# Hybrid attention layer on one core: in the first chunk, maxima and copies taken crosswise, one more upper part on ScalarE, one small transpose a unit later

## The chip, the cores and the metric

The kernel runs on one core of one Trainium2 chip. Its engines are TensorE (PE, matrix products, with PEld for its weight loads), VectorE (DVE), ScalarE (ACT), GpSimd (POOL) and SyncE (SP, which here only issues transfers). The metric is device time in microseconds of one execution, lower is better. Before the change the median of 3 runs is 1146.15 us (1145.9 to 1146.28).

## The reference, cut to what matters

One decoder layer over 2048 positions of width 1024. An adaLN vector (shift, scale, gate) comes from the condition `c`; the normalised input is scaled and shifted by it, projected once, and split over two attention branches.

```python
mod = jax.nn.silu(c) @ w_ada[l] + b_ada[l]
shift, scale, gate = jnp.split(mod, 3, axis=-1)
h = rms_norm(x, g_pre[l]) * (1.0 + scale[:, None, :]) + shift[:, None, :]
proj = h @ w_in[l]
qa, ka, va, fa, za, qb, kb, vb, zb = jnp.split(proj, split_points, axis=-1)
oa = forgetting_attention(qa, ka, va, fa + b_fgate[l]) * jax.nn.silu(za)
ob = sliding_window_sink_attention(rope(qb), rope(kb), vb, sinks[l]) * jax.nn.silu(zb)
y = jnp.concatenate([oa, ob], axis=-1) @ w_out[l]
x = x + gate[:, None, :] * rms_norm(y, g_post[l])
```

The change touches how `shift` becomes a column layout, how the first 512 rows of `h` are split into halves of lower precision, and when a maximum over the `zb` weights is gathered. What is computed stays the same.

## The kernel before, in words

Products keep nearly float32 precision with float16 operands: each operand is an upper part (`hi`, float16) and a rest (`lo`), and each product is three matmuls, hi by hi, hi by lo, lo by hi. The input is cut into four chunks of 512 rows (`ci` 0 to 3). For each chunk `turn(ci, k)` does one of eight column blocks: PE transposes four 128x128 tiles of the normalised rows into a PSUM bank `px`; ACT writes the scaled and shifted block as float32 (`hf`), and, where `high` is set, once more as float16 (the upper part, `hi`); else DVE makes the upper part by a cast (line 436). DVE then subtracts to get the rest (line 437). There are five `px` banks and three `hf` buffers. Both parts land in `hT[ci]`, which the projections read.

Ahead of it the start section runs in one fixed order per engine. `ada_two` multiplies the condition by `w_ada` into two PSUM banks, one for each half of 512 columns of the shift row (`pm[0][0]` is bank 1, `pm[0][1]` is bank 2). Line 628 takes the largest magnitude of each half on DVE, `ada_row` (line 512) copies each half out on ACT, `ada_turn` (line 516) transposes each half back **into the same bank** on PE, and `ada_col` (line 520) reads the transposed columns on DVE. The two maxima are joined (line 631), summed over quadrants by a matmul with `sel` (line 636), and give a bound `bm` (line 641), a power of two `pH`, and from it the scale `Gp` and shift `Shp` that every `turn` of chunk 0 needs.

Beside the turns DVE finds the maxima of the weights `zb0` and `zb1` (lines 659, 660). `z_row` and `z_all` gather them over the partitions with a transpose (line 997), a reduction (998), a scaling (999), a matmul (1002) and a copy to `mxs` (1003), all through bank 2. They hang on a list of units: unit n is the n-th group of projection matmuls. Units 0 to 7 are the `kb` projection of chunk 0 (line 335), 8 to 15 its `vb` projection (line 776, two 128-row blocks in bank 1, then two in bank 2), then come `zb0` and `zb1`. `at_slice(n, f)` issues `f` just ahead of unit n.

While that runs, ACT takes the sums of squares of chunk 1 (`squares(1)`, line 406), DVE makes its reciprocal root (`root(1)`, lines 92 to 106, at unit 9), and the rotary part of `kb` starts with a copy `qf` on ACT (line 723) and a product with the cosine on DVE (line 742). Each engine works off its instructions in order; two engines never read or write the same PSUM bank without a semaphore between them, reads included.

Of the kernel before, what the change touches and what calls it, by code (L numbers as in the profile page):

```python
# [15 lines left out]
ALU = mybir.AluOpType  # L16
AX = mybir.AxisListType
# [23 lines left out]
def hybrid_layer(  # L41
# [17 lines left out]
    V, A, G, PE, SP = nc.vector, nc.scalar, nc.gpsimd, nc.tensor, nc.sync  # L59
# [360 lines left out]
    def turn(ci, k):  # L420

        px = ps_x.tile([P, CH], F32, tag="x", name="px")
        for u in range(4):
            PE.transpose(px[:, u * P:(u + 1) * P], xt[ci * 4 + u][:, k * P:(k + 1) * P], ident[:])
        hf = hst.tile([P, CH], F32, tag="hf", name="hf")
        hi, lo = hT[ci][:, 0, k, :], hT[ci][:, 1, k, :]

        high = k % 2 == 0 if ci else k in (0, 4)

        def scaled():  # L430
            for dst in ([hi] if high else []) + [hf[:]]:
                A.activation(dst, px[:], AF.Identity, scale=Gp[:, k:k + 1], bias=Shp[:, k:k + 1])

        def split():
            if not high:
                V.tensor_copy(hi, hf[:])
            V.tensor_tensor(lo, hf[:], hi, op=ALU.subtract)

        return scaled, split

    def turn_x(ci, k):
        scaled, split = turn(ci, k)
        after(1, scaled)
        after(2, split)
# [12 lines left out]
    with tc.manual_schedule():  # L457
# [43 lines left out]
        pm = {1: [ps_x.tile([P, CH], F32, tag="x", name="pm") for _ in range(2)], 0: [bk[1], bk[2]]}  # L501
# [9 lines left out]
        def ada_row(half, n):  # L511
            A.activation(arow[half][:, n * CH:(n + 1) * CH], pm[half][n][:], AF.Copy)
# [112 lines left out]
            ada_two(0, k)  # L625
        rm = st.tile([P, 2], F32, name="rm")
        for n in range(2):
            V.tensor_reduce(rm[:, n:n + 1], pm[0][n][:], axis=AX.X, op=ALU.max, apply_absolute_value=True)
            ada_row(0, n)
        rmx = st.tile([P, 1], F32, name="rmx")  # L630
        V.tensor_reduce(rmx[:], rm[:], axis=AX.X, op=ALU.max)
        shf = col8("shf")
        turned = [turn(0, 0)]
        ada_turn(0, 0)
        turned.append(turn(0, 1))
        PE.matmul(bk[0][:, P:P + 1], sel[:], rmx[:], start=True, stop=True)
        ada_turn(0, 1)
# [352 lines left out]
    def at_slice(n, f):  # L990
        events.setdefault(n, []).append(f)
# [12 lines left out]
        for n in range(2):  # L1004
            wq[f"zb{n}"].append(mxs[:, 2 + n:3 + n])

    at_slice(8, z_row)
    at_slice(11, z_all)
    at_slice(9, lambda: root(1))
    for u in range(4):  # L1010
# [775 lines left out]
```

## Time and profile before

| what | value |
|---|---|
| median of 3 runs | 1146.15 us |
| the profiled execution's own time | 1144.82 us |
| its span | 1143.0 us |
| mean granted TensorE clock | 0.992 |
| DVE busy | 938.0 us (82%) |
| ACT busy | 692.2 us (61%) |
| POOL busy | 252.2 us (22%) |

The span is what the trace covers; 1.82 us of the execution's own time lie around it. Rows of the timeline give start and duration in us, engine, line, operation, tiles, a count, and in brackets how long the engine stood idle before and what released it. Starts are exact; the ends of matmuls are modelled, and two instructions of one engine can overlap a little where neither waits for the other.

### The profile page before, as it was taken

What the parts mean: (1) busy time and instruction counts of PE and PEld (TensorE: products, weight loads), DVE (VectorE), ACT (ScalarE), POOL (GpSimd) and SP (SyncE); (2) the same over time, 40 slices, a digit from 0 to 9 for tenths busy, and PEclk for the clock granted to TensorE, in tenths of its full rate; (3) what the DMA queues carried; (4) which work ended last, traced back from release to release, by engine and by line L of the source; (5) the groups of instructions that cost most, each with busy time, mean ns of one, the idle gap of its engine ahead of it and who ended that gap; (6) DMA issues with size and microseconds to landing.
All of it is one profiled execution on the core that took longest, in us unless ns stands there. A gap on an engine that the chain in (4) does not pass through costs nothing.

```text
span 1143.0 us, 26952 instructions
## 1 busy us (share of the span) xinstructions
PE 1102.7 (96%) x10386; PEld 638.2 (56%) x10386; DVE 938.0 (82%) x2331; ACT 692.2 (61%) x1177; POOL 252.2 (22%) x391
## 2 busy tenths in 40 slices
PE   5899999999999999999999999999999999999997
PEld 1466657654579855555555555555555554544443
DVE  6775668879899658789988889979888888988885
ACT  4666446656666534767767667777777677433331
POOL 2011122434443301122221221202111036100000
PEclk9999999999999999999999999999999998999999
DMA  9646426676787532343332332223212168478753
GB/s 332 224 139 171 106 71 135 117 159 126 153 164 141 108 66 71 71 100 81 75 78 70 98 85 64 62 54 87 52 40 61 29 167 216 131 186 215 192 163 111
DMA packets 210324, 136.35 MB, mean 119 GB/s; under 512 B 145276, under 2 KB 189348, under 8 KB 210196
## 3 DMA queue, kind: packets, MB, share of 16 engines
q1 hardware_dynamic: 198100, 98.53, 36.9%
q0 software_dynamic: 11616, 35.58, 11.1%
q8 instruction: 81, 1.33, 0.5%
q10 hardware_dynamic: 480, 0.53, 0.2%
q14 instruction: 47, 0.39, 0.1%
HBM read 62.58 MB, written 25.18 MB: 77 GB/s over the span
## 4 chain that ended last, share of the span: by engine, by line
PE 74%; DVE 11%; ACT 5%; DMA 5%; issue 4%; SPq 1%; POOL 0%; DVEq 0%; ACTq 0%; POOLq 0%
PE bk L335 28%; PE bk L1540 13%; PE bk L353 6%; PE sta L1345 5%; PE bk L1296 4%; PE sta L1346 4%; PE poa L1373 2%; PE poa L1374 2%; PE poa L1371 2%; DMA wa<-in_w_ada_dram 2%; PE bk L776 1%; DVE pha L1361 1%; PE pss L870 1%; PE pob L933 1%; DVE a_m L1299 1%
## 5 line engine op out<-in xcount | busy, mean ns | idle before, releaser
L1350 ACT ACTIVATE p<-sta,lift,scl_qk 128x1024 f32<-128x1024 f32 (+2 forms) x160 | 171.8, 1073 | 85.2 <-PE sta L1346 80.6
L335 PE MATMUL bk<-hT,wh_qk 128*128 128x512 f16 x768 | 198.0, 379 | 0.0
L1361 DVE TENSOR_TENSOR pha<-p,pha 128x1024 f16<-128x1024 f32 (+2 forms) x160 | 172.3, 1077 | 0.0
L1540 PE MATMUL bk<-wohl,oz 128*128 128x512 f16 (+2 forms) x792 | 170.2, 373 | 1.9 <-DVE wohl L1469 1.4
L1358 ACT ACTIVATE pha<-p 128x1024 f16<-128x1024 f32 (+2 forms) x160 | 148.2, 926 | 31.2 <-POOL p L1354 27.0
L1299 DVE TENSOR_REDUCE a_m<-bk 128x1 f32<-128x512 f32 x192 | 129.4, 683 | 36.7 <-PE bk L1296 36.2
L1540 PEld LDWEIGHTS <-oz 128*128 128x128 f16 x792 | 76.1, 99 | 87.3 <-issue 2.0
L1371 PE MATMUL poa<-vt,pha 128*128 128x65 f16 x1088 | 117.2, 193 | 2.1 <-DVE ona L1380 2.1
L1374 PE MATMUL poa<-vt,pha 128*128 128x65 f16 x1088 | 116.6, 193 | 0.8 <-DVE pha L1361 0.8
L1373 PE MATMUL poa<-vt,pha 128*128 128x64 f16 x1088 | 117.0, 195 | 0.0
L1345 PE MATMUL sta<-T 128*128 128x512 f16 (+1 forms) x320 | 109.9, 348 | 5.2 <-ACT p L1350 5.0
L1296 PE MATMUL bk<-T 66*128 66x512 f16 (+2 forms) x320 | 110.6, 349 | 0.9 <-DVE a_m L1301 0.5
L1371 PEld LDWEIGHTS <-pha 128*128 128x128 f16 x1088 | 101.9, 97 | 16.5 <-DVE ona L1380 2.9
L1373 PEld LDWEIGHTS <-pha 128*128 128x128 f16 x1088 | 101.4, 97 | 13.6
L335 PEld LDWEIGHTS <-wh_qk 128*128 128x128 f16 x768 | 70.1, 97 | 69.4 <-issue 0.6
L1346 PE MATMUL sta<-T 69*128 69x512 f16 (+1 forms) x320 | 108.3, 349 | 0.0
L1374 PEld LDWEIGHTS <-pha 128*128 128x128 f16 x1088 | 101.2, 99 | 1.2 <-DVE pha L1361 1.2
L335 PE MATMUL bk<-hT,wh_za 128*128 128x512 f16 x384 | 101.5, 382 | 0.0
L353 PE MATMUL bk<-wh_va,hT 128*128 128x128 f16 x1536 | 92.6, 219 | 0.0
L335 PE MATMUL bk<-hT,wh_zb 128*128 128x512 f16 x384 | 90.8, 379 | 0.0
L353 PEld LDWEIGHTS <-hT 128*128 128x128 f16 x1536 | 87.5, 98 | 4.9 <-issue 2.5
L1354 POOL TENSOR_SCALAR_AFFINE_SELECT p<-p 128x256 f32<-128x256 f32 x64 | 32.1, 502 | 258.1 <-ACT p L1350 247.4
(504 smaller groups left out, 1955.6 us busy)
## 6 DMA issues: line engine op xcount, KB each, us to landing
hT<-in_x_dram SPq DMA_DIRECT2D x20, 512.0 KB
wa<-in_w_ada_dram SPq DMA_DIRECT2D x16, 512.0 KB
T<-stq SPq DMA_DIRECT2D x128, 64.0 KB
T<-z_d SPq DMA_DIRECT2D x16, 512.0 KB
z_d<-tz POOLq DMA_DIRECT2D x30, 256.0 KB, 3.0
out_dram<-hT POOLq DMA_DIRECT2D x15, 512.0 KB, 5.7
xt<-in_x_dram SPq DMA_DIRECT2D x12, 512.0 KB
qs<-qf SPq DMA_DIRECT2D x80, 64.0 KB
```

Of the source, the lines that this page charges most:

```text
L335: PE.matmul(ps, whl[:, a, k, :], hT[ci][:, b, k, :], start=(k == 0 and n == 0), stop=(k == KT - 1 and n == 2))
L353: PE.matmul(ps[:, u * P:(u + 1) * P], hT[ci][:, a, k, u * P:(u + 1) * P], whl[:, b, k, :], start=(k == 0 and n == 0), stop=(k == KT - 1 an ...
L1296: PE.matmul(mx[:, :w], T[0:XM, 0, i * P:(i + 1) * P], T[0:XM, 2, pc * CH:pc * CH + w], start=True, stop=True)
L1345: PE.matmul(self.st[:, o:o + w], T[:, 3, kb_], T[:, 1, qc], start=True, stop=False)
L1346: PE.matmul(self.st[:, o:o + w], T[0:XR, 2, kb_], T[0:XR, 0, qc], start=False, stop=True)
L1350: A.activation(self.p32[:, :self.w], self.st[:, :self.w], AF.Exp, scale=scl[f"qk{self.hd}"][:], bias=lift[:])
L1358: A.activation(self.ph[:, 0, :self.w], self.p32[:, :self.w], AF.Copy)
L1361: V.tensor_tensor(self.ph[:, 1, :self.w], self.p32[:, :self.w], self.ph[:, 0, :self.w], op=ALU.subtract)
L1371: PE.matmul(po[:, u, :], ph[:, 0, pq], vt[:, b, hd, 0:65], start=(self.first and n == 0 and u == 0), stop=False)
L1373: PE.matmul(po[:, u, 0:64], ph[:, 0, pq], vt[:, b, hd, 65:VW], start=False, stop=False)
L1374: PE.matmul(po[:, u, :], ph[:, 1, pq], vt[:, b, hd, 0:65], start=False, stop=(self.last and n == len(self.blocks) - 1))
L1540: PE.matmul(py, self.hl[:, i, k, :], w_slot(8 * j + k)[:, cc], start=(k == 0 and m_ == 0), stop=(k == KT - 1 and m_ == 2))
```

## The change

Three edits. In `turn`, chunk 0 makes the upper parts of blocks 0, 3 and 6 on ACT, before of blocks 0 and 4. The maxima of the shift row are taken second half first, while the copies stay first half first. `z_row` hangs on unit 9, before on unit 8.

```diff
-        high = k % 2 == 0 if ci else k in (0, 4)
+        high = k % 2 == 0 if ci else k in (0, 3, 6)
...
         for n in range(2):
-            V.tensor_reduce(rm[:, n:n + 1], pm[0][n][:], axis=AX.X, op=ALU.max, apply_absolute_value=True)
+            V.tensor_reduce(rm[:, 1 - n:2 - n], pm[0][1 - n][:], axis=AX.X, op=ALU.max, apply_absolute_value=True)
             ada_row(0, n)
...
-    at_slice(8, z_row)
+    at_slice(9, z_row)
     at_slice(11, z_all)
     at_slice(9, lambda: root(1))
```

In the rows below `bk_139` is bank 1 and `bk_140` bank 2; the brackets name the engines whose semaphores an instruction waits for.

On PE, after the last products of `ada_two`, before the change: the last transpose of `turn(0, 0)`, the first half's `ada_turn`, the start of `turn(0, 1)`.

```order
L424 MATMUL px<-ident,xt_257 128x128 [waits Activation_49]
L516 MATMUL bk_139<-ident,arow_209 128x128 [waits Activation_49]
L516 MATMUL bk_139<-ident,arow_209 128x128 x3
L424 MATMUL px<-ident,xt_251 128x128
L424 MATMUL px<-ident,xt_253 128x128
```

The same place on PE after the change.

```order
L424 MATMUL px<-ident,xt_257 128x128 [waits Activation_49]
L516 MATMUL bk_139<-ident,arow_209 128x128 [waits DVE_49]
L516 MATMUL bk_139<-ident,arow_209 128x128 x3
L424 MATMUL px<-ident,xt_251 128x128
L424 MATMUL px<-ident,xt_253 128x128
```

The order is the same, but the first half's transposes wait for DVE, no longer for ACT. On DVE at that place, after the change:

```order
L628 TENSOR_REDUCE rm<-bk_140 128x1 [waits PE_49]
L628 TENSOR_REDUCE rm<-bk_139 128x1 [waits Activation_49]
L631 TENSOR_REDUCE rmx<-rm 128x1 [waits DVE_49]
L520 TENSOR_REDUCE shf<-bk_139 128x4 [waits PE_49]
L641 TENSOR_TENSOR bm<-bk_138,pre 128x1 [waits PE_49]
```

Bank 1 is read by ACT first and by DVE second, bank 2 the other way round; before, DVE read each bank first.

On ACT, the end of chunk 0's turns and what follows (`junk` is a square of chunk 1, `qf` the copy for the rotary part), with the change's rows marked:

```order
 L406 ACTIVATE junk_520,ss_516<-hT3_110 128x1024
 L406 ACTIVATE junk_522,ss_516<-hT3_110 128x1024
+L723 ACTIVATE qf_594<-bk0_138 128x512
 L406 ACTIVATE junk_524,ss_516<-hT3_110 128x1024
-L723 ACTIVATE qf_594<-bk0_138 128x512
 L416 ACTIVATE hT3_110<-hT3_110,rst_517 128x1024
```

`qf` has moved ahead of the last square of chunk 1. On PE, at the border between `kb` (line 335) and `vb` (line 776):

```order
 L335 LDWEIGHTS wh_kb_365
 L335 MATMUL bk0_138<-hT0_107,wh_kb_365 128x512
-L997 MATMUL bk2_140<-ident_120,mxs_130 2x128
 L776 LDWEIGHTS hT0_107
 L776 MATMUL bk1_139<-wh_vb_367,hT0_107 128x136
```

The transpose of the two weight maxima leaves this place and stands twelve `vb` matmuls later. SP and POOL keep their rows in the same order.

## The prediction

> **What bounds the kernel now.** I read the page's span and its chain of work first, then the waits and the timeline of the first 80 us, where all three edits lie.
>
> ```profile
> span 1143.0 us, 26952 instructions
> PE 74%; DVE 11%; ACT 5%; DMA 5%; issue 4%; SPq 1%; POOL 0%; DVEq 0%; ACTq 0%; POOLq 0%
> ```
>
> Three quarters of the chain that ended last are PE. From about 80 us on the chain hardly leaves PE, so what the first 80 us lose or gain moves the end by about as much. In there PE waits for others. The place of the second edit, engine by engine (DVE, ACT, PE):
>
> ```profile
> 36.83 0.69 DVE L628 TENSOR_REDUCE rm<-bk 128x1 f32<-128x512 f32 x1 [4.34 <-PE bk L508]
> 37.69 0.69 DVE L628 TENSOR_REDUCE rm<-bk 128x1 f32<-128x512 f32 x1 [0.17 <-PE bk L508]
> 38.41 0.15 DVE L631 TENSOR_REDUCE rmx<-rm 128x1 f32<-128x2 f32 x1
> 39.45 0.16 DVE L641 TENSOR_TENSOR bm<-bk,pre 128x1 f32<-128x1 f32 x1 [0.31 <-PE bk L636]
> 37.55 0.60 ACT L512 ACTIVATE arow<-bk 128x512 f32<-128x512 f32 x1 [3.23 <-DVE rm L628]
> 38.41 0.60 ACT L512 ACTIVATE arow<-bk 128x512 f32<-128x512 f32 x1 [0.26 <-DVE rm L628]
> 40.68 0.78 ACT L432 ACTIVATE hT<-px,Shp,Gp 128x512 f16<-128x512 f32 x1 [1.67 <-DVE shf L520]
> 37.58 0.66 PE L424 MATMUL px<-ident,xt 128*128 128x128 f32 x4
> 38.20 0.66 PE L516 MATMUL bk<-ident,arow 128*128 128x128 f32 x4
> 39.13 0.28 PE L636 MATMUL bk<-rmx,sel 128*128 128x1 f32 x2
> ```
>
> By what releases the two maxima, bank 1 is ready at 36.8 and bank 2 at 37.65. The chain runs: maximum of half 1, its copy (37.55), its transposes (38.20), the four of turn 1, the matmul with `sel`, `bm` at 39.45, first turned block at 40.68. Soon after it DVE becomes full. The first row is a stretch of 5 us (length, busy time and count of PE, PEld, DVE, ACT, POOL, granted clock, DMA share, GB/s), the others are DVE's timeline:
>
> ```profile
> 45.00:50.00 5.00, 3.33 (x14) 1.16 (x12) 4.90 (x10) 4.85 (x9) 0.00 (x0) 1.00 0.11 28
> 43.29 0.69 DVE L437 TENSOR_TENSOR hT<-hf,hT 128x512 f16<-128x512 f32 x1
> 43.90 0.42 DVE L436 CAST hT<-hf 128x512 f16<-128x512 f32 x1
> 44.35 0.69 DVE L437 TENSOR_TENSOR hT<-hf,hT 128x512 f16<-128x512 f32 x1
> 47.69 1.21 DVE L659 TENSOR_REDUCE mxs<-wr_zb 128x1 f32<-128x1024 f32 x1
> 48.82 0.42 DVE L436 CAST hT<-hf 128x512 f16<-128x512 f32 x1
> 50.33 0.69 DVE L437 TENSOR_TENSOR hT<-hf,hT 128x512 f16<-128x512 f32 x1
> 50.94 1.21 DVE L660 TENSOR_REDUCE mxs<-wr_zb 128x1 f32<-128x1024 f32 x1
> 52.97 0.15 DVE L92 TENSOR_SCALAR rs_v<-ss 128x4 f32<-128x4 f32 x1
> 56.71 0.15 DVE L1003 COPY mxs<-bk 128x2 f32<-128x2 f32 x1
> ```
>
> DVE is busy for 4.90 of 5 us. A cast costs it 0.45 us (43.90 to 44.35), a subtraction 0.61, a maximum of weights 1.13 (47.69 to 48.82). The root of chunk 1 starts at 52.97, `mxs` is copied at 56.71; on that hang the scale of the `zb0` weights, DVE's and ACT's work behind it, and so the turns of chunk 1. What closes the stretch:
>
> ```profile
> 78.94 0.38 PE L335 MATMUL bk<-hT,wh_kb 128*128 128x512 f16 x1 [0.39 <-DVE hT L436]
> 79.67 0.59 PE L335 MATMUL bk<-hT,wh_kb 128*128 128x512 f16 x2 [0.35 <-DVE hT L437]
> ```
>
> PE, on the last block of chunk 1's turns, waits 0.39 and 0.35 us for DVE. So the line over DVE and ACT sets the end of this stretch, and PE has about 0.7 us in hand against it.
>
> **The change part by part.** The sum is made against the profiled execution, 1144.82 us (span 1143.0 and 1.82 around it). It lies 1.33 under the median of 1146.15; I carry the difference over to the median.
>
> *Crosswise maxima.* ACT no longer waits for DVE: it copies half 1 from 36.83 on, 0.72 earlier, done at 37.43. DVE takes half 2 first, when bank 2 is ready, 37.69 as before. Then half 1: two reads in a row without a wait between them are 0.61 apart for this length (43.29 to 43.90), so from 38.30 to 38.99. Half 1's maximum is now the last reader of bank 1, and the order of the changed kernel shows the transposes into bank 1 waiting for DVE. They start at about 39.03 (0.04 for a hand-over, as from 38.15 to 38.20), not 38.20: **+0.83**. The joined maximum is ready at 39.02 + 0.15 = 39.17, before PE has come to the `sel` matmul, so it adds nothing. Behind the waiting transposes PE queues turn 1, `sel`, half 2's transposes and turns 2 to 4; `bm` waits for `sel`, and all turned blocks of chunk 0 wait for `bm`. From 38.20 to 40.68 nothing else in the chain changes, so the whole section moves by 0.83. If those transposes were not held, they could start once turn 0's four are through, no earlier than 38.0, and the `sel` matmul would still need the later maximum, 39.17 plus a hand-over of 0.04, which is 0.1 over its 39.13: the bounds are +0.1 and +0.9, and I take +0.83, since the wait stands in the order.
>
> [...]
>
> *Upper parts on ACT.* Blocks 3 and 6 lose their casts on DVE, block 4 gains one: of six, five are left. Counted from an unmoved start, up to the first weight maximum DVE has four casts before and after, so it starts at 47.69 as before. Block 6 then goes straight to its subtraction: from there DVE is 0.45 early, the last rest of chunk 0 starts at 49.88, the second weight maximum at 50.49. ACT makes eleven parts of chunk 0 (eight `hf`, three upper) where it made ten:
>
> ```profile
> 44.01 0.80 ACT L432 ACTIVATE hT<-px,Shp,Gp 128x512 f16<-128x512 f32 x1
> 44.67 0.80 ACT L432 ACTIVATE hf<-px,Shp,Gp 128x512 f32<-128x512 f32 x1
> 47.56 1.05 ACT L406 ACTIVATE junk<-hT 128x1024 bf16<-128x1024 f32 x1
> 51.10 1.06 ACT L406 ACTIVATE junk<-hT 128x1024 bf16<-128x1024 f32 x1
> 52.06 0.19 ACT L406 ACTIVATION_READ_ACCUMULATOR junk<-hT 128x1 f32 x1
> 52.16 0.58 ACT L723 ACTIVATE qf<-bk 128x512 f32<-128x512 f32 x1
> ```
>
> One part takes 0.66 (44.01 to 44.67). Ten from 40.68 would be through at 47.28, but the squares start at 47.56, so 0.28 are waits for DVE to free an `hf` buffer; with DVE's casts further apart these go. Eleven end at 47.94, and the squares start 0.4 later. In the changed order `qf` stands ahead of the fourth square: it starts 1.06 after the third one, as before after the fourth, and takes 0.48 (0.58 less the 0.1 by which rows overlap on ACT), where two squares are 1.18 apart: 1.54 - 1.18 = 0.36 more. The sum, ready before at 52.06 + 0.19 = 52.25, is ready at 53.01, and the root cannot start before 53.05, against 52.97: **+0.08**. So DVE's saved cast is no gain at the root. Without ACT's delay the root would be up to 0.4 earlier; with a full 0.66 and a `qf` of 0.58 it is 0.4 later. These are the bounds; I take +0.08, the sum of the rows.
>
> *`z_row` a unit later.* PE's rows at the border of the two projections:
>
> ```profile
> 51.08 0.59 PE L335 MATMUL bk<-hT,wh_kb 128*128 128x512 f16 x2 [0.25 <-DVE hT L437]
> 52.21 0.27 PE L997 MATMUL bk<-ident,mxs 128*2 128x128 f32 x1 [0.54 <-DVE mxs L660]
> 52.32 2.29 PE L776 MATMUL bk<-wh_vb,hT 128*128 128x136 f16 x36
> 54.85 0.88 PE L776 MATMUL bk<-wh_vb,hT 128*128 128x136 f16 x12
> 56.91 3.00 PE L776 MATMUL bk<-wh_vb,hT 128*128 128x136 f16 x48 [1.18 <-DVE mxs L1003]
> ```
>
> PE loses the wait of 0.54 and starts `vb` at 51.05, 1.27 early. Twelve matmuls of 0.064 (2.29 over 36) take it to 51.81, where the weight maxima have just come in (51.7), so the transpose waits for nothing. But the second half of `vb` needs bank 2 back, which `mxs` frees at line 1003, and that stands on DVE behind the root. So what PE wins at 52 it waits out before 56.91: the gain is **0**, bounded by 0 and -0.54, the wait taken away; 0 because the next wait on the same bank is longer. PE's pause there grows to about 2.4 us. The order of SP and POOL is unchanged, and `qf` comes 0.1 later in real time, with more than 2 us of DVE work between it and its use.
>
> Sum: 0.83 + 0.08 + 0 = **+0.91 us**. After 58 us all waits are between the same instructions, so all of it should reach the end: the profiled execution at 1145.73, the median at **1147.1**. That is 0.08%, and I call a change measurable here from 0.2%, which is 2.3 us.
>
> **Rivals.** *A, the hand-over pays.* The transposes in effect do not lose by the wait (+0.1), and DVE's saved cast reaches the root (-0.4): 1146.15 - 0.3 = **1145.85**. For it: DVE has no pause in this stretch, and the copy does start 0.72 earlier. Against it: the wait for DVE on bank 1 and the fourth square behind `qf`. It decides at line 516: where its first transpose starts, at 38.0 or 39.0 in a trace.
>
> *B, slower: PE's longer pause halves its clock.* The trace has such a case:
>
> ```profile
> 25.92 0.27 PE L589 MATMUL bk<-ident,mx 128*1 128x128 f32 x1 [1.91 <-DVE mx L614]
> 20.00:26.00 6.00, 3.47 (x18) 1.00 1.02 409
> 26.00:33.00 7.00, 6.39 (x20) 0.51 1.03 408
> 33.00:40.00 7.00, 6.72 (x38) 1.00 1.07 380
> 50.00:60.00 10.00, 8.01 (x106) 1.00 0.27 61
> ```
>
> The columns of the last four are stretch, length, PE busy, granted clock, DMA share, GB/s. After a pause of 1.91 us the clock is at half until 33; the pause of 1.18 before 56.91 did nothing. A pause of 2.4 lies above the first. At half clock the 48 matmuls of 3.00 us after it take 3.0 more, less the 0.7 in hand: +2.3, to **1149.4**; if only half of them are hit, 1.5 less 0.7, to 1147.9. Where it decides: a pause of some 2 us that ends under a clock of 0.5. Against it: work of full density lies close on both sides, and the times of before repeat within 0.4 us.
>
> [...]
>
> **How the numbers follow.** The forecast, +0.91, has 0.72; its bounds together run from -0.8 (0.1 - 0.4 - 0.5) to +1.3 (0.9 + 0.4). A has 0.12, B 0.12, and 0.04 is left for what I do not see. The range is 1145.3 to 1148.9: the lower end is the lower bound and takes in A, the upper goes past +1.3 (1147.5) into the milder half of B. Faster by over 0.2% needs 1143.9, outside all cases: 0.03. Slower by over 0.2% begins at 1148.4: most of B and a little more, 0.10. The rest, 0.87, is within 0.2%.
>
> **What would show it.** Right: line 512's first copy released by PE near 36.85; line 516's first group released by DVE `rm` near 39.0; the first line 432 near 41.5; the root at line 92 released by ACT's square, at about 53.9; line 1003 at about 57.6, and a PE pause over 2 us before `vb`'s second half. Wrong: line 516 still near 38.2, a root that waits for DVE work only, a clock under 1.00 between 55 and 65, or a shift at 80 us that is not there at the end.

## The result and the profile after

| | before | after |
|---|---|---|
| median of the runs taken side by side (22 each) | 1146.34 us | 1148.72 us |
| lowest and highest of them | 1145.25, 1149.24 | 1146.77, 1150.78 |
| the profiled execution's own time | 1144.82 us | 1147.56 us |
| its span | 1143.0 us | 1145.8 us |
| mean granted TensorE clock | 0.992 | 0.993 |

The change makes the kernel slower by a ratio of 1.0018 (95% interval 1.0013 to 1.0024), about 2.1 us; the two medians are 2.38 us apart. The forecast was +0.91 us. The time lies inside the range, the sign is the forecast one, and the size is more than twice what the sum gave and beyond the sum's own upper bound of +1.3.

The first stretch went as the sum had it. Timeline of the kernel after, DVE, ACT and PE at the crosswise maxima:

```profile
37.90 1.29 DVE L628 TENSOR_REDUCE rm<-bk 128x1 f32<-128x512 f32 x2 [5.72 <-PE bk L508]
37.04 0.60 ACT L512 ACTIVATE arow<-bk 128x512 f32<-128x512 f32 x1 [3.02 <-PE bk L508]
41.73 0.78 ACT L432 ACTIVATE hT<-px,Shp,Gp 128x512 f16<-128x512 f32 x1 [2.51 <-DVE shf L520]
39.24 0.66 PE L516 MATMUL bk<-ident,arow 128*128 128x128 f32 x4 [0.80 <-DVE rm L628]
```

ACT copies half 1 as soon as PE has filled bank 1, and PE's transposes into that bank are released by DVE's later maximum, at 39.24 instead of 38.20. Bank 1 itself was filled 0.21 us later here (its first reader starts at 37.04, before at 36.83; over all traces here that start lies between 36.67 and 37.39), so the edit's own part is 1.04 - 0.21 = 0.83.

What was not foreseen stands twenty microseconds on. ACT, DVE, POOL and PE of the kernel after:

```profile
53.92 0.19 ACT L406 ACTIVATION_READ_ACCUMULATOR junk<-hT 128x1 f32 x1
54.14 0.17 DVE L92 TENSOR_SCALAR rs_v<-ss 128x4 f32<-128x4 f32 x1 [0.49 <-ACT junk L406]
57.21 1.76 DVE L418 TENSOR_SCALAR hT<-hT,rst 128x1024 f32<-128x1024 f32 x1
58.89 0.15 DVE L1003 COPY mxs<-bk 128x2 f32<-128x2 f32 x1
58.96 0.74 DVE L418 TENSOR_SCALAR hT<-hT,rst 128x1024 f32<-128x1024 f32 x1
57.15 1.27 POOL L735 TENSOR_TENSOR qs<-qs,sinT 128x512 f32<-128x512 f32 x1 [48.65 <-DMA qs<-qf]
59.09 4.39 PE L776 MATMUL bk<-wh_vb,hT 128*128 128x136 f16 x48 [3.47 <-DVE mxs L1003]
```

The same two lines in the kernel before:

```profile
56.05 0.74 DVE L418 TENSOR_SCALAR hT<-hT,rst 128x1024 f32<-128x1024 f32 x1
56.78 0.74 DVE L418 TENSOR_SCALAR hT<-hT,rst 128x1024 f32<-128x1024 f32 x1
56.81 1.84 POOL L735 TENSOR_TENSOR qs<-qs,sinT 128x512 f32<-128x512 f32 x1 [48.28 <-DMA qs<-qf]
```

Two things are new. DVE's first row scaling of chunk 1 (line 418, which stands between the root and line 1003) took 1.76 us where it took 0.74. It starts 0.06 after GpSimd's product with the sine (line 735), which is released by the transfer of the copied `qf` (it starts 4.66 after ACT's copy at 52.49, before 4.65 after the one at 52.16). Before, DVE's first row was over when GpSimd started, 0.76 behind it. GpSimd came 0.03 behind DVE's second row instead, and GpSimd's row was the long one, 1.84. And PE's pause ahead of the second half of `vb` is 3.47 us, where 1.18 was and some 2.4 were expected, and the 48 matmuls behind it took 4.39 us, not 3.00. The clock of those stretches (columns as in the prediction), and then what closes the stretch on PE:

```profile
56.00:59.00 3.00, 0.00 (x0) 0.00 (x0) 2.82 (x7) 2.48 (x4) 1.27 (x1) 0.94 0.47 108
59.00:62.00 3.00, 2.91 (x27) 2.91 (x27) 2.24 (x10) 1.19 (x2) 0.00 (x0) 0.50 0.41 93
62.00:65.00 3.00, 3.00 (x34) 2.33 (x33) 2.85 (x11) 1.08 (x3) 0.00 (x0) 1.00 0.75 243
```

```profile
82.22 0.38 PE L335 MATMUL bk<-hT,wh_kb 128*128 128x512 f16 x1 [0.35 <-DVE hT L436]
82.94 0.59 PE L335 MATMUL bk<-hT,wh_kb 128*128 128x512 f16 x2 [0.35 <-DVE hT L437]
```

The clock is at half from 59 to 62 and full again after; the 0.94 of the row ahead says that it fell shortly before 59. The last two products of `kb` for chunk 1 start at 82.94, before at 79.67. The page's chain of work, followed back from the end, covers only the last sixth of the span in this trace, so the stretch is read from the timeline alone.

For what follows I use one **local figure**: from the start of the first reader of bank 1 to the start of those last two products. It leaves out how early or late that first reader starts (36.67 to 37.39 in the traces here). Before it is 79.67 - 36.83 = 42.84, after 82.94 - 37.04 = 45.90: 3.06 us more.

### The profile page after: what moved, and what is told of

Its sections match the earlier page's. It is cut to its first block, busy times and chain, and to the rows that moved or that the text cites. A ratio compares the mean times of both kernels' runs of the same rounds, so it can differ in the third digit from the quotient of the medians.

```text
span 1145.8 us, 26949 instructions
## 1 busy us (share of the span) xinstructions
PE 1102.8 (96%) x10386; PEld 638.1 (56%) x10386; DVE 939.1 (82%) x2330; ACT 693.2 (60%) x1178; POOL 252.3 (22%) x391
## 5 line engine op out<-in xcount | busy, mean ns | idle before, releaser
L1354 POOL TENSOR_SCALAR_AFFINE_SELECT p<-p 128x256 f32<-128x256 f32 x64 | 34.6, 540 | 257.9 <-ACT p L1350 242.9
```

## The experiments

**The theory.** Four terms make up the 3.06: the crosswise maxima (about 0.85); ACT's fourth square behind `qf` (about 0.1); DVE held off by GpSimd at line 418, because the upper parts put `qf` early and the root late (about 1.0); and the halved clock after a pause which those three and the moved transpose lengthen together (about 1.1). **The rivals** were that one of the other two edits alone brings the loss, that line 418 is long for a reason that has nothing to do with GpSimd, and that the halved clock is covered, because PE would wait for DVE later anyway. In the expectations T is the theory and R with a number is a rival. Each run below is timed in five rounds against the kernel before on the same chip, and its figure is from its profiled execution.

| run | what it is | local figure | line 418 | PE's pause | 48 matmuls | ratio to before (95%) |
|---|---|---|---|---|---|---|
| before | | 42.84 | 0.74 | 1.18 | 3.00 | |
| after | all three edits | 45.90 | 1.76 | 3.47 | 4.39 | 1.0018 (1.0013 to 1.0024) |
| e1_swap | crosswise maxima alone | 43.69 | 0.74 | 1.17 | 3.00 | 1.0005 (0.9996 to 1.0014) |
| e2_upper | upper parts alone | 45.32 | 1.77 | 2.78 | 4.62 | 1.0019 (1.0010 to 1.0029) |
| e3_zrow | moved transpose alone | 42.88 | 0.74 | 1.89 | 3.00 | 1.0010 (1.0001 to 1.0019) |
| e4_noswap | after without crosswise maxima | 45.31 | 1.75 | 3.46 | 4.63 | 1.0028 (1.0019 to 1.0038) |
| e5_pool | after, GpSimd held back | 45.00 | 0.74 | 2.46 | 4.51 | 1.0010 (1.0001 to 1.0019) |
| e6_busy | after, PE kept busy | 44.82 | 1.76 | 1.32 | 3.00 | 1.0007 (0.9999 to 1.0016) |
| e7_both | after, both | 43.79 | 0.74 | 0.29 | 3.00 | 1.0001 (0.9992 to 1.0010) |
| e8_zpx | after, gather in a `px` bank | 46.21 | 1.76 | none here | not apart | 1.0017 (1.0008 to 1.0026) |
| f1_sel | before, `sel` product earlier | 42.45 | 0.75 | 1.18 | 3.00 | 1.0000 (0.9991 to 1.0009) |
| f2_early | before, gather earlier | 43.33 | 1.28 | none | not apart | 1.0002 (0.9993 to 1.0011) |
| f3_early_sel | both of these | 42.94 | 1.29 | none | not apart | 1.0003 (0.9994 to 1.0012) |

### One edit at a time

**e1_swap**: the kernel before with the crosswise maxima alone.

```diff
-            V.tensor_reduce(rm[:, n:n + 1], pm[0][n][:], axis=AX.X, op=ALU.max, apply_absolute_value=True)
+            V.tensor_reduce(rm[:, 1 - n:2 - n], pm[0][1 - n][:], axis=AX.X, op=ALU.max, apply_absolute_value=True)
```

> Before, with the crosswise maxima alone. Figure used in all runs: from the first reader of bank 1 (start of the first line 628 or 512 there) to the start of the last two kb products of chunk 1 (line 335 x2 at the end of the wait for DVE): 42.84 us before (36.83 to 79.67), 45.90 after (37.04 to 82.94). Theory T (the +3.06 are four parts: transposes held by DVE 0.83; a fourth square behind qf 0.1; the first line 418 stretched by GpSimd's line 735 from 0.74 to 1.76, 1.0; a PE pause of 3.5 us that halves the clock, about 1.1): only the first part, figure 43.7, line 418 at 0.74, clock 1.00 between 55 and 65. Rival R1 (all of it follows from the later start of chunk 0): figure 45.9.

Measured 43.69, 0.85 more than before. ACT, DVE, POOL and PE of its timeline:

```profile
37.12 0.60 ACT L512 ACTIVATE arow<-bk 128x512 f32<-128x512 f32 x1 [3.04 <-PE bk L508]
57.18 0.74 DVE L418 TENSOR_SCALAR hT<-hT,rst 128x1024 f32<-128x1024 f32 x1
57.96 1.82 POOL L735 TENSOR_TENSOR qs<-qs,sinT 128x512 f32<-128x512 f32 x1 [49.45 <-DMA qs<-qf]
80.81 0.59 PE L335 MATMUL bk<-hT,wh_kb 128*128 128x512 f16 x2 [0.35 <-DVE hT L437]
```

The edit moves DVE and GpSimd alike, so DVE still starts 0.78 ahead of GpSimd, as before (0.76), and its row stays at 0.74. The 0.85 pass whole from 39 us to 81 us. The crosswise maxima cost what the sum said, and they don't bring the rest.

**e2_upper**: the kernel before with the upper parts alone.

```diff
-        high = k % 2 == 0 if ci else k in (0, 4)
+        high = k % 2 == 0 if ci else k in (0, 3, 6)
```

> Before, with the upper parts of blocks 0, 3 and 6 on ACT alone. qf stands ahead of the fourth square in the order. Theory T: line 735 on GpSimd and the first line 418 start within 0.1 us of each other, so line 418 is stretched to about 1.7, mxs is copied 1.1 later, PE's pause ahead of the second half of vb grows to 2.3 to 2.6 us and may halve the clock: figure 43.9, or 45.0 with the clock. R1: 42.4 to 42.9, since DVE has a cast less. R2 (line 418 is slow through the data it reads, not through GpSimd): line 418 at 0.74, figure 42.9.

Measured 45.32, or 2.48 more. POOL, DVE and PE:

```profile
56.25 1.26 POOL L735 TENSOR_TENSOR qs<-qs,sinT 128x512 f32<-128x512 f32 x1 [47.75 <-DMA qs<-qf]
56.29 1.77 DVE L418 TENSOR_SCALAR hT<-hT,rst 128x1024 f32<-128x1024 f32 x1
58.18 4.62 PE L776 MATMUL bk<-wh_vb,hT 128*128 128x136 f16 x48 [2.78 <-DVE mxs L1003]
59.00:62.00 3.00, 3.00 (x33) 3.00 (x31) 2.27 (x9) 1.15 (x1) 0.00 (x0) 0.57 0.34 79
```

This one edit, priced at 0.08, brings the long row of DVE, the longer pause and the halved clock by itself. GpSimd is first by 0.04 us.

**e3_zrow**: the kernel before with the moved transpose alone.

```diff
-    at_slice(8, z_row)
+    at_slice(9, z_row)
```

> Before, with z_row a unit later alone. Theory T: vb starts 0.6 us earlier, PE waits that out before its second half (pause 1.8), mxs is copied as before, clock 1.00, figure 42.8 plus or minus 0.1. Rival R3 (the pause alone, moved to one place, halves the clock): clock at 0.5 for some us after 57, figure above 43.3.

Measured 42.88. PE and its clock:

```profile
57.50 3.00 PE L776 MATMUL bk<-wh_vb,hT 128*128 128x136 f16 x48 [1.89 <-DVE mxs L1003]
59.00:62.00 3.00, 3.00 (x36) 2.24 (x34) 2.26 (x7) 1.38 (x3) 0.24 (x1) 1.00 0.27 61
```

What PE wins at the border it waits out later, 1.89 - 1.18 = 0.71 more, at a full clock. The price 0 holds in this execution. The ratio of the whole run, 1.0010, is just off 1 by its interval; a clock halved in some other executions could make that (the granted clock is 0.9937 on average over its eleven executions, 0.9942 over the 31 of the kernel before beside them), but single executions of either lie between 0.992 and 0.996, so it is not shown.

**e4_noswap**: the changed kernel with the maxima back in their old order.

```diff
-            V.tensor_reduce(rm[:, 1 - n:2 - n], pm[0][1 - n][:], axis=AX.X, op=ALU.max, apply_absolute_value=True)
+            V.tensor_reduce(rm[:, n:n + 1], pm[0][n][:], axis=AX.X, op=ALU.max, apply_absolute_value=True)
```

> After, with the maxima in the old order (upper parts and z_row changed). Theory T: 0.83 less than after, figure 45.1 with the clash at line 418, the pause of 3.4 us and the halved clock; 44.0 where the clock stays at 1.00. R1: 42.8.

Measured 45.31, 0.59 less than after. DVE and PE:

```profile
56.16 1.75 DVE L418 TENSOR_SCALAR hT<-hT,rst 128x1024 f32<-128x1024 f32 x1
58.04 4.63 PE L776 MATMUL bk<-wh_vb,hT 128*128 128x136 f16 x48 [3.46 <-DVE mxs L1003]
```

Most of the crosswise maxima's 0.85 goes away and the rest of the loss stays. The 0.24 between 0.83 and 0.59 are in the 48 matmuls, 4.63 here and 4.39 in after: the low clock covers more of them. In the whole run the 0.59 is not seen (1.0028, an interval that overlaps that of after). The granted clock is 0.9913 on average over its ten executions and 0.9927 over the 22 of after; where in the run that difference lies was not traced.

### Taking the two new costs away

**e5_pool**: the changed kernel with a small copy of `mxs` on GpSimd, written behind line 1003 and so ahead of line 735 in GpSimd's order. GpSimd then cannot start line 735 before DVE has passed its first line 418.

```diff
-    dz = const.tile([2, 3], F32, name="dz")
+    dz = const.tile([2, 3], F32, name="dz"); zcp = const.tile([P, 2], F32, name="zcp")
...
-        V.tensor_copy(mxs[:, 2:4], bk[2][:, P:P + 2])
+        V.tensor_copy(mxs[:, 2:4], bk[2][:, P:P + 2]); G.tensor_copy(zcp[:], mxs[:, 2:4])
```

> After, with a two-column copy of mxs on GpSimd (issued with z_all) ahead of its product line 735, so that this product starts behind line 1003 and no longer beside the first line 418. Theory T: the first line 418 takes 0.74, mxs is copied 1.0 earlier than in after, PE's pause shrinks to about 2.4 us; figure 44.9 with a halved clock, 43.8 without. R2 (line 418 is slow through its data): line 418 stays at 1.7, figure 45.9.

Measured 45.00. POOL, DVE and PE:

```profile
57.81 0.64 POOL L1003 COPY zcp<-mxs 128x2 f32<-128x2 f32 x1 [49.21 <-DVE mxs L1003]
58.41 1.26 POOL L735 TENSOR_TENSOR qs<-qs,sinT 128x512 f32<-128x512 f32 x1
56.93 0.74 DVE L418 TENSOR_SCALAR hT<-hT,rst 128x1024 f32<-128x1024 f32 x1
57.80 4.51 PE L776 MATMUL bk<-wh_vb,hT 128*128 128x136 f16 x48 [2.46 <-DVE mxs L1003]
```

With GpSimd out of the way DVE's row is 0.74 again and the pause 1.01 shorter. The instruction and its data are the same, so the long row was GpSimd's doing. The clock is still halved, after 2.46 us.

**e6_busy**: the changed kernel with ten products of the size of `kb`'s in PE's pause, into a `px` bank. Their result is not read.

```diff
-    dz = const.tile([2, 3], F32, name="dz")
+    dz = const.tile([2, 3], F32, name="dz"); busy = lambda w_: [PE.matmul(w_[:], wq["kb"][:, 0, 0, :], hT[0][:, 0, 0, :], start=True, stop=True) for _ in range(10)]
...
-    at_slice(11, z_all)
+    at_slice(11, z_all); at_slice(12, lambda: busy(ps_x.tile([P, CH], F32, tag="x", name="px")))
```

> After, with ten added kb products (their result is not read) on PE between the two halves of vb, in the pause, into a px bank. Theory T: line 418 still 1.76, the pause shrinks to about 1.3 us, the clock stays at 1.00 between 55 and 65, the second half of vb takes 3.0 and not 4.39; figure 44.8. R4 (the halved clock costs nothing, since DVE and ACT set the end): figure stays at 45.9.

Measured 44.82. DVE, PE and the clock:

```profile
56.87 1.76 DVE L418 TENSOR_SCALAR hT<-hT,rst 128x1024 f32<-128x1024 f32 x1
55.12 2.32 PE L994 MATMUL px<-hT,wh_kb 128*128 128x512 f16 x10
58.76 3.00 PE L776 MATMUL bk<-wh_vb,hT 128*128 128x136 f16 x48 [1.32 <-DVE mxs L1003]
59.00:62.00 3.00, 3.00 (x49) 2.69 (x46) 2.24 (x10) 1.35 (x3) 0.00 (x0) 1.00 0.40 90
```

DVE's row is as long as after, and line 1003 comes no earlier; only the pause is cut to 1.32 by products that nothing needs. The clock stays at 1.00, the 48 matmuls take 3.00, and the figure falls by 1.08. So the halved clock is not covered: it reaches 81 us.

**e7_both**: the edits of e5_pool and e6_busy together.

> After, with both: the copy on GpSimd and the ten added products. Theory T: line 418 at 0.74, clock 1.00, figure 43.8: what is left over before is the 0.83 of the held transposes and 0.1 of the fourth square.

Measured 43.79. DVE and PE:

```profile
57.30 0.74 DVE L418 TENSOR_SCALAR hT<-hT,rst 128x1024 f32<-128x1024 f32 x1
58.17 3.00 PE L776 MATMUL bk<-wh_vb,hT 128*128 128x136 f16 x48 [0.29 <-DVE mxs L1003]
80.92 0.59 PE L335 MATMUL bk<-hT,wh_kb 128*128 128x512 f16 x2 [0.35 <-DVE hT L437]
```

What is left over the crosswise maxima alone (43.69) is 0.10, the place of the fourth square. The whole run is back at the kernel before, 1.0001 (0.9992 to 1.0010), while after it was 1.0018.

**e8_zpx**: the changed kernel with lines 997 to 1003 through a `px` bank and not bank 2, so that the second half of `vb` need not wait for line 1003.

```diff
-        PE.transpose(bk[2][0:2, 0:P], mxs[:, 2:4], ident[:])
+        zp[0] = ps_x.tile([P, CH], F32, tag="x", name="px"); PE.transpose(zp[0][0:2, 0:P], mxs[:, 2:4], ident[:])
...
```

The lines left out here put `zp[0]` for `bk[2]` in lines 998, 1002 and 1003.

> After, with the gathering of the two weight maxima (lines 997 to 1003) in a px bank, not in bank 2, so that the second half of vb does not wait for mxs. Theory T: no PE pause of over 1 us there, clock 1.00, line 418 still 1.76 beside line 735, figure 44.8. R4: 45.9.

A miss: 46.21, no better than after. PE, and the stretch behind:

```profile
54.45 3.72 PE L776 MATMUL bk<-wh_vb,hT 128*128 128x136 f16 x60
61.21 0.60 PE L335 MATMUL bk<-hT,wh_zb 128*128 128x512 f16 x2 [3.03 <-ACT wh_zb L273]
62.00:65.00 3.00, 3.00 (x11) 1.68 (x12) 2.82 (x12) 1.31 (x3) 0.00 (x0) 0.62 0.92 328
```

`vb` now runs through without a pause, and PE then waits 3.03 us for the `zb0` weights, whose scale hangs on the same line 1003; behind that pause the clock is low again (0.62). The bank held back only the second half of `vb`. The next work needs the gathered maximum itself, so freeing the bank puts the pause behind `vb` and takes nothing away.

### Looking for a faster version

**f1_sel**: the kernel before with line 636 ahead of `turn(0, 1)`.

```diff
-        turned.append(turn(0, 1))
         PE.matmul(bk[0][:, P:P + 1], sel[:], rmx[:], start=True, stop=True)
+        turned.append(turn(0, 1))
```

> The kernel before, with the product on line 521 written ahead of the four transposes of line 516 for bank 1, so that PE issues it as soon as the joint maximum is there and not behind four transposes of 0.66 us together. Nothing else is moved. Theory: PE reaches the product about 0.4 us earlier than in the kernel before, because the transposes then run beside VectorE's work on its result; the first copy of line 432 starts 0.4 us earlier and the local figure (first reader of bank 1 to the start of the last two products of the first weight on chunk 1) is 42.4 to 42.6 instead of 42.84. Rival: the wait for the transposed row decides line 520 and 432 anyway; the figure stays at 42.8 to 42.9. The whole run by the theory: 0.2 to 0.4 us below before, which the runs can hardly tell from no change.

The expectation describes the edit inexactly: the product is that of line 636, and it moves ahead of turn 1's transposes, not ahead of those of line 516. Measured 79.17 - 36.72 = 42.45, as the theory had it; the run, 1.0000, cannot tell 0.4 us.

**f2_early**: the kernel before with the gather two units earlier and the root one unit later.

```diff
-                        events.setdefault(n + 9, []).append(f)
+                        events.setdefault(n + 7, []).append(f)
...
-    at_slice(11, z_all)
-    at_slice(9, lambda: root(1))
+    at_slice(9, z_all)
+    at_slice(10, lambda: root(1))
...
-        at_slice(10 + u, lambda u=u: normal(1, (u,)))
+        at_slice(11 + u, lambda u=u: normal(1, (u,)))
```

> The kernel before, with the maxima gathered and spread earlier: line 1002 two units earlier, the first write weight scaled two units earlier on VectorE and ScalarE, and the root and the row scalings of the next chunk one unit later. Theory: the wait on line 1003 is what holds the second half of the value products, so a product and copy that come before the root take the pause of 1.18 us in PE away, and the clock stays at 1.00; the local figure falls by 0.5 to 1.2 us, to 41.6 to 42.3. Rival 1: VectorE's root now ends later and with it ScalarE's row scalings, so the copies out of px wait instead and the figure stays within 0.3 of 42.84. Rival 2: VectorE's row scaling (line 418) falls beside GpSimd's line 735 and both are held; figure 43.5 to 44.

Measured 80.32 - 36.99 = 43.33, above what the theory and the first rival gave and 0.17 under the second rival's range. DVE, POOL and PE:

```profile
53.70 0.16 DVE L1003 COPY mxs<-bk 128x2 f32<-128x2 f32 x1 [0.49 <-PE bk L1002]
57.52 1.28 DVE L418 TENSOR_SCALAR hT<-hT,rst 128x1024 f32<-128x1024 f32 x1
56.97 1.27 POOL L735 TENSOR_TENSOR qs<-qs,sinT 128x512 f32<-128x512 f32 x1 [48.51 <-DMA qs<-qf]
53.60 5.14 PE L776 MATMUL bk<-wh_vb,hT 128*128 128x136 f16 x84
```

PE's pause is gone, at a full clock. But the root ends later, and DVE's row scaling meets line 735 again, which is 0.55 ahead of it.

**f3_early_sel**: f1_sel and f2_early together.

> Both edits of the two runs before this one together, on the kernel before. Theory: the two gains are at different places (39 us and 57 us) and add up: figure 41.2 to 41.9, the whole run 0.5 to 1.5 us below before. Rival: whatever is gained at 39 us is waited for again at 57 us, and the figure equals that of the earlier gather alone.

Measured 79.93 - 36.99 = 42.94, 0.39 under f2_early: the gain at 39 us adds on, as the theory said, but its figure of 41.2 to 41.9 was missed by what f2_early lacked. None of the eleven is measurably faster than the kernel before.

## Why the prediction was right in sign and too small

- **Crosswise maxima, +0.83:** right, in place and in size (0.83 at line 516 of after, 0.85 in e1_swap at the end of the stretch). Rival A's hand-over did not pay.
- **Upper parts, +0.08 at the root:** the terms that were counted are right (the root is released by ACT's last square, and 0.10 remains in e7_both). What failed is the sentence behind the sum, "After 58 us all waits are between the same instructions, so all of it should reach the end", together with the step from the root to line 1003, which the prediction let run as before. Two instructions that wait for nothing of each other stand there: the edit brings `qf`, and with it GpSimd's line 735, forward against DVE's line 418, and the crosswise maxima don't. The order of starts turned from DVE 0.76 ahead to GpSimd 0.06 ahead, and DVE's row grew from 0.74 to 1.76. The mis-sized term measures 44.82 - 43.79 = 1.03 (e6_busy less e7_both). The prediction did follow `qf`, and its 0.1 was right (GpSimd starts 0.34 later in after, of which 0.21 come from bank 1), but it held it only against DVE's use of it and not against DVE's other work beside GpSimd. The sign stood in the trace of before: line 735 took 1.84 us at 56.81, where its twenty there have a median of 1267 ns. The view of that one line (count, shortest, median and longest in ns, first and last start):

```profile
L735 POOL TENSOR_TENSOR qs<-qs,sinT x20: 1257/1267/2057, 56.8 to 344.1; 128x512 f32<-128x512 f32 x20
```

- **`z_row`, 0:** right by itself (42.88 against 42.84). Its share is the longer pause, 0.71 us of it in e3_zrow.
- **Rival B, the halved clock, at 0.12:** this happened. The pause was put at 2.4 us and came to 3.47, since line 1003 was later by DVE's long row. The clock costs 45.90 - 44.82 = 1.08 (after less e6_busy). That is between nothing and the 2.3 that rival B gave if all 48 matmuls are hit: they took 1.39 more, as in its milder case (1.5), of which about 0.3 were in hand, not 0.7. The two waits that the prediction read as PE's reserve, 0.39 and 0.35, are still 0.35 and 0.35 in after, so they gave up next to nothing; 0.24 of the 0.3 lie in the 21 products ahead of them (4.94 before, 4.70 after). The other pair of runs, 45.00 - 43.79 (e5_pool less e7_both), gives 1.21 for a pause of 2.46, which is the length that the prediction itself had worked out. So the chance of 0.12 was too low even without DVE's long row. One reason given against B, that the times of before repeat within 0.4 us, rested on three runs; the 22 of the result spread over 4 us.
- **The sum:** 0.85 + 0.10 + 1.03 + 1.08 = 3.06, which is the whole of the local figure. Of it the profiled spans show 2.8 at the end and the ratio of the runs 2.1 (1.5 to 2.8). Where up to half a microsecond or more is made good between 83 us and the end was not traced. The same holds for the runs' ratios: they follow the local figure roughly (2.1 us less in e7_both than in after, and 1.0001 for 1.0018), but differences under 1 us stay inside their intervals. The low clock is not peculiar to the profiled executions: over all executions the granted clock averages 0.9927 in after (22 runs) and 0.9917 in e2_upper (10), against 0.9943 in e6_busy, 0.9939 in e7_both (11 each) and 0.9942 in the kernel before, timed beside these (31 and 33). A stretch of 3.4 us at half clock would lower that average by 0.0015 (an estimate: 3.4 x 0.5 out of 1146).
- **The range:** that the time falls inside it is partly luck. Its upper end, 1148.9, was drawn for the milder half of rival B; the 1.03 at line 418 was in no term, and the median of 1148.72 leaves 0.18 to spare.

## What to carry to other kernels

When an edit shifts two engines by different amounts, look for instructions of VectorE and GpSimd that ran close beside each other before, as lines 418 and 735 did here, and ask which of them will now start first; a row that is much longer than its like (here 1.84 us against a median of 1.27) was the sign of it, and the order of waits showed nothing there. A late release can cost twice: behind each of the five pauses of PE of 2.46 to 3.47 us that were compared here the clock was halved as well, and in after that cost 1.08 us, so price the pause with the clock behind it. And before a buffer is put in to shorten a wait, follow the waited-for value itself: if the next work needs it too, the pause only moves, as in e8_zpx (3.03 us behind `vb`, 3.47 inside it in after).

## What the runs showed of the hardware that was not expected

Where lines 418 and 735 overlapped, the one that started second took longer than its like and ended after the other. In after GpSimd's row ends at 57.15 + 1.27 = 58.42 and DVE's at 57.21 + 1.76 = 58.97, 0.55 later; in e2_upper it is 57.51 and 58.06, in f2_early 58.24 and 58.80, though there DVE's row started 0.55 behind and not 0.06. So in these three DVE ended about 0.55 after GpSimd whatever its start, with rows of 1.76, 1.77 and 1.28 us where the row of before took 0.74. The other way round, GpSimd's row ended 1.13 after DVE's second row scaling: in before 56.78 + 0.74 = 57.52 and 56.81 + 1.84 = 58.65, and the same 1.13 in e1_swap, e3_zrow and f1_sel, with rows of 1.82 to 1.85 where the median of line 735 is 1.27. That the second one is held until the first has finished is a reading of these ends; what holds it was not shown.

PE's clock stayed at 1.00 after pauses of 1.18, 1.32 and 1.89 us between 54 and 62 us and fell to half with pauses of 2.46, 2.78, 3.03, 3.46 and 3.47 there, and with one of 1.91 near 25 us, where PE was busy for 3.47 of the 6 us from 20 to 26. These lengths are no limit for other places: in before a pause of 3.90 us ended at 8.51, and the clock was 1.00 in every stretch from 0 to 20.

The length of the pause does not settle when the clock falls. In after it fell while PE was still idle (stretch, length, PE busy and count, granted clock, DMA share, GB/s):

```profile
58.00:59.00 1.00, 0.00 (x0) 0.81 0.56 127
59.00:60.00 1.00, 0.91 (x9) 0.50 0.36 82
62.00:63.00 1.00, 1.00 (x19) 0.99 0.38 61
```

A mean of 0.81 is 0.38 us at half clock, so it fell at about 58.6 and rose at about 62.0. In e8_zpx the same reading (1.00 from 59 to 62, 0.62 from 62 to 65, 0.89 from 65 to 70) puts the fall at about 62.7, some 1.5 us after PE had gone back to work at 61.21. Worked out in this way, the low clock lasted about 3.4 us in all five traces that have it near 60 us: in after and e8_zpx from the stretches just named, in e2_upper from 0.86 and 0.57 (56 to 59 and 59 to 62), in e4_noswap from 0.90 and 0.53, in e5_pool from 0.76 and 0.67. The pause of 1.91 was followed by 6.8 us of it in before (0.70 from 26 to 26.5, 0.50 up to 33, 0.97 from 33 to 33.5) and by 3.4 in after (0.89 from 27.5 to 28, 0.50 up to 31, 0.70 from 31 to 31.5). So how many of the matmuls behind a pause are hit varies with something besides the pause, and after pauses of 3.47 and 3.46 the 48 took 4.39 in one trace and 4.63 in the other. Each of these is one profiled execution; near 57 us no pause lay between 1.89 and 2.46.
